# A modulation bias added by a product with the identity, and two SiLUs of keys moved behind the second mixer's values

## The chip, the core and the metric

The kernel runs on one core of a Trainium2 chip. The metric is the device time of one execution in microseconds (us), the median of the runs. The engines are named as in the profile: PE (matrix products; PEld is its weight load), DVE (vector), ACT (scalar functions), POOL (GpSimd) and SP (which issues the DMAs here). Each engine works through its own instructions in order and waits by semaphores for the others.

## What is computed

One layer on 256 latent tokens and 256 context tokens of width 1024: modulation by six vectors from a conditioning vector, two token mixers in parallel (a gated mLSTM with a short convolution on queries and keys, and an HGRN2 scan), a gated merge, and a mixture of experts (top 4 of 32). Cut to what the change touches:

```python
sh1, sc1, g1, sh2, sc2, g2 = split(silu(c) @ w_ada + b_ada, 6)      # late part: g1, sh2, sc2, g2
p = modulate(rmsnorm(x), sh1, sc1) @ w_in + b_in
mqk, mv, mo, hq, hi, hg, hf, ga, gb, mg = split(p)
mq, mk = split(silu(short_conv(mqk, conv_w)))                       # 4 heads each, 3x3 taps
mlstm(mq * 128 ** -0.5, mk, mv, mg)                                 # first mixer
hgrn(silu(hq), (1 - lb) * sigmoid(-hf), hi, log(lb + (1 - lb) * sigmoid(hf)))   # second mixer, 4 heads
```

## The kernel before

**Stages.** The first 280 us or so are the front: norms, the early modulation, and the products with `w_in`, done unit by unit. A unit is a weight tile of 1024 x 256 that is loaded, split into a high and a low part (the high part is the cast L226 on ACT, the low part the subtraction L228 on DVE, for three units on POOL), and multiplied in two blocks by three products each (L237). The units go in the order: queries 2 (first tile done before), `hf` 0, keys 0, `hf` 1, keys 1, `hi` 0, `hi` 1, `hf` 2, `hf` 3, first mixer's values `mv` 0 and 1, then the gates. A block's result stands in a PSUM bank until an engine copies it out; `mm_bank` hands out two banks named `mm` and one named `am` in turn, and only the two `mm` while the late modulation runs. So a block waits until the block two or three before it was copied out. `hi` has four blocks, copied out by DVE at L511.

**Key and query blocks.** `ev_conv` copies a block into an image on ACT and appends its convolution to the list `convs`; a convolution is 9 taps on DVE for queries and 9 + 3 for keys (L661 to L670). After each block the unit loop takes one convolution from `convs`. `silu_qk` (L738) first empties `convs` and then does the SiLU of all four heads of queries and keys: a sigmoid on ACT into `csg`, and a product on DVE (L749 for keys, L751 for queries).

**The second mixer's heads.** `hgrn_head` is a generator for one head; the unit loop advances it block by block, two heads with `hi` and `hf`, two with `mv`. A head runs scans on DVE (L534 to L542), 28 subtractions on DVE into X (L560, L561), the exponentials of X (L562), of G (L543) and of Y (L567 to L569) on ACT, products of Y on POOL (L570 to L572), of X on DVE and POOL (L582, L583), transposes `trh` (L588) and small products on PE. `last_heads` prepares heads 2 and 3: eight sigmoids, then `exp_table` orders the load of the table for exponentials and logarithms, then four logarithms (L516). `to_hgrn` does the same for heads 0 and 1, behind the SiLU.

**The late modulation.** `ada_rest` takes two halves of 8 weight tiles. For each it forms products in the bank `am` (L196), spread over the blocks from `hf` 2 on by the table `rest_at`, and DVE adds the bank to `ada_sb`, which holds the bias (L855). The second half uses the same bank and waits for that addition.

**What sets the order.** Outside the parts under `manual_schedule` the framework's scheduler orders each engine's instructions by its own estimates, so the position of an instruction follows from the built program, not from the text alone.

Of the kernel before, what the change touches and what calls it, by code (L numbers as in the profile page):

```python
# [12 lines left out]
AF = mybir.ActivationFunctionType  # L13
OP = mybir.AluOpType
# [3 lines left out]
P = 128  # L18
D = 1024
KB = 8  # L20
T = 256
NTOK = 512
HM = 4
# [41 lines left out]
def layer_kernel(ctx: ExitStack, tc, x, ctxt, w_ada, b_ada, n_mix_post, n_ffn_post, w_in, b_in, w_pa, w_pb, w_out,  # L65
                 w_router, b_router, w_gu, b_gu, w_dn, b_dn, consts, vecs, out, dbg=None):
    nc = tc.nc
# [13 lines left out]
    def bcast_rows(vec, n):  # L81
# [5 lines left out]
    ident = cp.tile([P, P], F32, name="ident")  # L87
# [35 lines left out]
    ada_sb = ctx.enter_context(tc.tile_pool(name="fa", bufs=1, side="right", reuse_waits="tile")).tile(  # L123
        [P, 2, 512], F32, name="ada_sb")
# [10 lines left out]
    qT = fp.tile([P, HM, T], F32, name="qT")  # L135
    kT = fp.tile([P, HM, NTOK], F32, name="kT")
# [19 lines left out]
    def raw_tile():  # L156
        return ringr.tile([P, 2048], F32, name="w", tag="w", bufs=2)
# [31 lines left out]
    def ada_load(c0, k):  # L189
        w = raw_tile()  # L190
        nc.sync.dma_start(w, w_ada[k * P:(k + 1) * P, c0:c0 + 2048])
        return w

    def ada_mm(bank, w, k):
        for j in range(4):
            nc.tensor.matmul(bank[32 * j:32 * j + 32, :], cs[:, k, :], w[:, 512 * j:512 * j + 512],  # L196
                             start=(k == 0), stop=(k == KB - 1), skip_group_check=True)

    banks = []

    def mm_bank():

        banks.append("mm" if len(banks) % 3 < 2 or ada_runs else "am")
        return pmm.tile([P, 512], F32, name="mm", tag=banks[-1], bufs=2 if banks[-1] == "mm" else 1)
# [78 lines left out]
    def after(instructions):  # L283

        stack = ExitStack()
        for i_ in () if in_order else instructions:
            stack.enter_context(tc.issue_after(i_.ins))
        return stack

    def exp_table(instructions):  # L290

        with after(instructions):
            ld = nc.scalar.preload_act_table_set("natural_log_exp_and_others")
        return after([ld])
# [150 lines left out]
    sig = []  # L445
# [46 lines left out]
    def silu_hq():  # L492
        for j in range(2):
            q2 = hqT[:, 2 * j:2 * j + 2]
            sg = hq_.tile([P, 2, T], F32, name="sg", tag="sg", bufs=1)
            with after(last_xs):
                sig.append(nc.scalar.activation(sg, q2, AF.Sigmoid))
            nc.gpsimd.tensor_tensor(q2, q2, sg, op=OP.mult)
# [16 lines left out]
    def log_f(r):  # L515
        nc.scalar.activation(lf[r], lf[r], AF.Ln, scale=olb[:, r:r + 1], bias=lb[:, r:r + 1])  # L516
        nc.vector.tensor_scalar(kk[r], kk[r], olb[:, r:r + 1], None, op0=OP.mult)

    def last_heads():
        sg2 = []  # L520
        with after(hexp):
            for r in (2, 6, 3, 7):
                sg2.append(nc.scalar.activation(kk[r], lf[r], AF.Sigmoid, scale=-1.0))
                sg2.append(nc.scalar.activation(lf[r], lf[r], AF.Sigmoid))
        estack.append(exp_table(sg2))
        for r in (2, 6, 3, 7):
            log_f(r)
        work.extend(hgrn_head(h) for h in (2, 3))
# [113 lines left out]
    convs = []  # L642
# [92 lines left out]
        nc.scalar.activation(gcol[:, 0:4], tg[:, 0:4], AF.Identity)  # L735
        nc.scalar.activation(gcol[:, 4:8], tg[:, 4:8], AF.Exp)

    def silu_qk():  # L738
        while convs:
            convs.pop(0)()  # L740
        sg = hq_.tile([P, 2, NTOK], F32, name="csg", tag="Y")
        n_ = 0
        for h in range(HM):
            for a, n, sc in ((qT[:, h], T, float(P) ** -0.5), (kT[:, h], NTOK, None)):
                g = sg[:, n_ % 2, 0:n]
                n_ += 1
                sig.append(nc.scalar.activation(g, a, AF.Sigmoid))
                if sc is None:
                    nc.vector.tensor_mul(a, a, g)  # L749
                else:  # L750
                    nc.vector.scalar_tensor_tensor(a, a, sc, g, op0=OP.mult, op1=OP.mult)  # L751

    def ev_v(cc):
        def ev(b, i):
# [90 lines left out]
    def ada_rest():  # L845
        for i in range(8):
            nc.gpsimd.dma_start(ada_sb[32 * (i % 4):32 * (i % 4) + 1, i // 4, :],
                                b_ada[2048 + 512 * i:2560 + 512 * i].rearrange("(a b) -> a b", a=1))
        for hf in range(2):
            b = pmm.tile([P, 512], F32, name="am", tag="am", bufs=1)  # L850
            for k in range(KB):
                ada_mm(b, ada_load(2048 + 2048 * hf, k), k)
                if k < KB - 1:
                    yield
            nc.vector.tensor_add(ada_sb[:, hf], ada_sb[:, hf], b)  # L855
            yield

    def block_of(a, k):
# [46 lines left out]

    def to_hgrn():
        silu_hq()
        silu_qk()
        estack.append(exp_table(sig))
        for r in (0, 4, 1, 5):  # L910
            log_f(r)
# [4 lines left out]
    def to_last():  # L916
        step(100)
        last_heads()
# [7 lines left out]
    for u in (mq_[1], hf_[0], mk_[0], hf_[1], mk_[1]):  # L926
        unit(*u)
    unit(*hi_[0], to_hgrn)
    unit(*hi_[1], None, first_heads)
    unit(*hf_[2])  # L930
# [46 lines left out]
    first = True  # L977
    for c0, n, cnt_ in ((HG, "hg", 2), (MO, "mo", 2), (GA, "ga", 4), (GB, "gb", 4)):
        for cc in range(cnt_):
            unit(win(c0 + 256 * cc), blocks_T(T, ev_gate(n, c0, 2 * cc), ev_gate(n, c0, 2 * cc + 1)),  # L980
                 to_late if first else head_norms if (n, cc) == ("gb", 2) else None)
            first = False
# [107 lines left out]
    def first_merge(i):  # L1090
# [3 lines left out]
              half(w_pb, 0, HM, 512, 512)]  # L1094
    rest_at = {(7, 0): 1, (7, 1): 1, (8, 0): 2, (8, 1): 2, (9, 0): 2, (9, 1): 3, (10, 0): 3, (10, 1): 2}
    rest = ada_rest()
    load_at = {(18, 0): ((first_gu, 0, 0), (first_gu, 0, 1),),
                (19, 0): ((first_gu, 1, 0),),
# [69 lines left out]
    for n_ in range(4):  # L1168
# [20 lines left out]
        g = (gga, ggb)[i]  # L1189
        blks = [slice(4 * q_ + 2 * j2, 4 * q_ + 2 * j2 + 2) for j2 in range(2)]  # L1190
        for j2, blk in enumerate(blks):
            b = mm_bank()
# [11 lines left out]
    a = L["aT"].rearrange("p i a k t -> p (i a k t)")  # L1204
# [641 lines left out]
    with tc.manual_schedule():  # L1846
# [5 lines left out]
        for ch in range(2):  # L1852
            ends[ch]()
            for hf in range(2):
                hs_ = slice(512 * hf, 512 * hf + 512)
                nc.vector.scalar_tensor_tensor(x1[:, ch, hs_], scr[2 * ch + hf], yss[:, 4 + ch:5 + ch], x1[:, ch, hs_],  # L1856
                                               op0=OP.mult, op1=OP.add)
# [48 lines left out]
```

## Time and profile before

| | |
|---|---|
| median of 3 runs | 1363.46 us (1362.53 to 1363.48) |
| profiled execution | 1364.41 us, span 1362.6 us |
| PE busy over the span | 1265.5 us (93%) |
| DVE, ACT, POOL busy | 561.8, 361.8, 129.6 us |
| granted TensorE clock, mean | 0.981 of full speed |
| bytes moved | 474.12 MB, mean 348 GB/s |

The span runs from the first to the last instruction. In a timeline an entry has its start, its length, engine, line, operation and tiles; `x8` means eight instructions in a row, and what stands in square brackets is the idle time of the engine just before, with what ended it. A PE length includes the time in the pipeline, so the next entry can start before the end. Instructions are in pairs on PE for a full fp32 product.

### The profile page before, as it was taken

Reading aid. Unit: us, or ns where it says so; the run is one execution under the profiler, and the core shown is the slowest. Engines: PE = TensorE matmul, PEld = TensorE weight load, DVE = VectorE, ACT = ScalarE, POOL = GpSimd, SP = SyncE. Lnnn points to the kernel's source line nnn. Section 1 sums busy time; section 2 is a strip of 40 time slices with the busy share of each in tenths; the row PEclk is TensorE's granted clock in tenths of the full one; section 3 lists DMA queues with packets and bytes.
Section 4 is the critical chain, followed back from the end, with each engine's and each line's share of the span. In section 5 each row is a group of like instructions: output and inputs, shape, how many; then the busy total and the mean of one; then the engine's idle time right before and its main releaser. Section 6 shows DMA issues by size and latency. Waiting matters only on the chain. (4 is left out here: it accounts for less than half of the span.)

```text
span 1362.6 us, 20982 instructions
## 1 busy us (share of the span) xinstructions
PE 1265.5 (93%) x8719; PEld 637.9 (47%) x8719; DVE 561.8 (41%) x1211; ACT 361.8 (27%) x712; POOL 129.6 (10%) x140
## 2 busy tenths in 40 slices
PE   4998877999998899999999999999999999999995
PEld 2788665799993333333333333333333333333321
DVE  4699477787666332322222222222222222222224
ACT  3557362446643321111111111211121111211102
POOL 4543335300110000000000000000000000000000
PEclk9999988999999899999999999999999999999997
DMA  9731625745889989999999999999999999999994
GB/s 324 242 102 63 202 78 195 260 135 195 309 304 395 390 367 422 430 424 427 427 427 427 425 392 429 426 426 426 429 424 427 426 428 427 425 428 426 427 420 163
DMA packets 78424, 474.12 MB, mean 348 GB/s; under 512 B 6048, under 2 KB 45480, under 8 KB 50672
## 3 DMA queue, kind: packets, MB, share of 16 engines
q1 hardware_dynamic: 77936, 472.54, 85.7%
q8 instruction: 70, 1.15, 0.3%
q14 instruction: 34, 0.28, 0.1%
q0 software_dynamic: 384, 0.15, 0.0%
HBM read 471.60 MB, written 1.07 MB: 347 GB/s over the span
## 5 line engine op out<-in xcount | busy, mean ns | idle before, releaser
L1609 PE MATMUL pg<-wc,hmh 128*64 128x512 f32 x1048 | 271.8, 598 | 14.9 <-DMA wc<-in_w_gu_dram 14.4
L1609 PE MATMUL pu<-wc,hmh 128*64 128x512 f32 x1048 | 268.9, 592 | 0.0
L1659 PE MATMUL dnl<-wc,hmh 128*64 128x512 f32 x1056 | 236.0, 598 | 9.4 <-ACT hmh L1640 9.1
L1659 PEld LDWEIGHTS dnl<-wc,hmh 128*64 128x64 f32 x1056 | 73.6, 137 | 169.1 <-issue 135.4
L1651 DVE TENSOR_TENSOR ys<-dnl,ys 128x512 fp32r<-128x512 f32 x32 | 22.1, 692 | 307.2 <-ACT ys L1650 307.2
L1609 PEld LDWEIGHTS pu<-wc,hmh 128*64 128x64 f32 x1048 | 74.4, 137 | 150.5 <-issue 150.5
L1620 ACT ACTIVATE scr<-scr 128x512 f32<-128x512 f32 (+1 forms) x34 | 21.0, 619 | 465.8 <-DVE scr L1619 465.8
L1609 PEld LDWEIGHTS pg<-wc,hmh 128*64 128x64 f32 x1048 | 66.9, 136 | 145.5 <-issue 107.4
L1675 DVE SCALAR_TENSOR_TENSOR xr<-sc,wv,xr 128x512 f32<-128x512 f32 x124 | 87.4, 747 | 109.5 <-PE sc L1669 109.5
L1619 DVE TENSOR_SCALAR scr<-pg 128x512 f32<-128x512 f32 (+1 forms) x34 | 22.9, 676 | 219.7 <-PE pg L1609 219.7
L237 PE MATMUL mm<-xh,wp 128*128 128x256 f32 (+1 forms) x576 | 107.7, 332 | 4.2 <-DVE hi_sb L511 3.1
L237 PEld LDWEIGHTS mm<-xh,wp 128*128 128x128 f32 x576 | 88.0, 196 | 14.8 <-issue 4.1
L1385 ACT ACTIVATE hmh<-xp,s2c,a2c 128x64 f32<-128x64 f32 x264 | 81.5, 414 | 38.6 <-PE xp L1581 33.2
L1717 POOL TENSOR_TENSOR scr<-xr,g2n 128x512 f32<-128x512 f32 x2 | 2.5, 1266 | 908.2 <-issue 908.2
L1650 ACT CAST ys<-dnl 128x512 fp32r<-128x512 f32 x32 | 18.7, 585 | 232.3 <-PE dnl L1659 232.3
L1581 PEld LDWEIGHTS <-hb 128*128 128x128 bf16 x960 | 43.7, 98 | 24.3 <-issue 24.3
L228 DVE TENSOR_TENSOR wp<-w,wp 128x2048 fp32r<-128x2048 f32 x21 | 48.0, 2288 | 13.4 <-ACT wp L226 13.4
L237 PE MATMUL mm<-xl,wp 128*128 128x256 f32 (+1 forms) x288 | 53.2, 328 | 0.0
L1669 PE MATMUL sc<-ys,ohT 64*128 64x512 f32 x256 | 48.3, 450 | 4.0 <-DVE xr L1673 3.1
L226 ACT CAST wp<-w 128x2048 fp32r<-128x2048 f32 x25 | 47.5, 1900 | 15.6 <-PE mm L237 8.1
L1581 PE MATMUL xp<-oh,hb 128*128 128x64 bf16 x960 | 47.2, 193 | 0.0
L237 PEld LDWEIGHTS mm<-xl,wp 128*128 128x128 f32 x288 | 44.4, 196 | 4.2
(625 smaller groups left out, 1529.4 us busy)
## 6 DMA issues: line engine op xcount, KB each, us to landing
wc<-in_w_gu_dram SPq DMA_DIRECT2D x119, 2048.0 KB, 25.2
wc<-in_w_dn_dram SPq DMA_DIRECT2D x63, 2048.0 KB, 25.2
w<-in_w_in_dram SPq DMA_DIRECT2D x26, 1024.0 KB, 5.3
w<-in_w_ada_dram SPq DMA_DIRECT2D x16, 1024.0 KB, 4.9
wc<-in_w_gu_dram SPq DMA_DIRECT2D x16, 1024.0 KB, 27.0
aw<-in_w_ada_dram SPq DMA_DIRECT2D x8, 1024.0 KB, 11.7
w<-in_w_pa_dram SPq DMA_DIRECT2D x2, 1024.0 KB, 5.3
w<-in_w_out_dram SPq DMA_DIRECT2D x2, 1024.0 KB, 6.6
```

The source lines that it names most:

```text
L226: nc.scalar.copy(hi, w)
L228: eng.tensor_tensor(lo, w, hi.bitcast(F32), op=OP.subtract)
L237: nc.tensor.matmul(o, ls[k][a], rs[k][b], start=(i + k == 0), stop=(i == 2 and k == n - 1))
L1385: nc.scalar.activation(xg[:, k], xp[k], AF.Identity, scale=a2c[:, k:k + 1], bias=s2c[:, k:k + 1])
L1581: nc.tensor.matmul(xp[:, k], part[:, ch, k * P:(k + 1) * P], oh[:, ch], start=(i == 0), stop=(i == 5))
L1609: nc.tensor.matmul(banks[u][n * g:n * g + n, :], xg[:, k], rows_[:, c0:c0 + W], start=False, stop=(k == KB - 1), skip_group_check=True)
L1619: nc.vector.tensor_scalar(g_, cut(banks[0], i), 7.0, None, op0=OP.min)
L1620: nc.scalar.activation(s_, g_, AF.Sigmoid, scale=1.702)
L1651: nc.vector.tensor_sub(ys[1], b, ys[0].bitcast(F32))
L1659: nc.tensor.matmul(b[64 * hf:64 * hf + 64, :], aT_[:, j, g], dn[g][:, j, hf * 512:hf * 512 + 512], start=(g == 0 and j == 0), stop=(g == 1 ...
L1669: nc.tensor.matmul(s[hf], ohT[ps_, ch * P:(ch + 1) * P], ys[i][ps_], start=(i == 0), stop=(i == 1))
L1675: nc.vector.scalar_tensor_tensor(dst, s[hf], wv[:, ch, col:col + 1], dst, op0=OP.mult, op1=OP.add)
```

## The change

1. In `ada_rest` a product of `ada_sb` with the identity (`ident`) opens the accumulation in the bank, so that the bias stands in it; the 8 weight tiles' products add to it, and ACT copies the bank to `ada_sb`. DVE's addition is gone.
2. `silu_qk` takes the heads to be done. `to_hgrn` leaves the last two convolutions in `convs`, and does the SiLU of four queries and of keys 0 and 1. `last_heads` takes what is left in `convs`, and does the SiLU of keys 2 and 3 behind its sigmoids and before the table load.

```diff
-    def ada_mm(bank, w, k):
+    def ada_mm(bank, w, k, first=True):
         for j in range(4):
             nc.tensor.matmul(bank[32 * j:32 * j + 32, :], cs[:, k, :], w[:, 512 * j:512 * j + 512],
-                             start=(k == 0), stop=(k == KB - 1), skip_group_check=True)
+                             start=(first and k == 0), stop=(k == KB - 1), skip_group_check=True)
...
                 sg2.append(nc.scalar.activation(lf[r], lf[r], AF.Sigmoid))
+            while convs:
+                convs.pop(0)()
+            silu_qk((), range(2, HM), sg2)
         estack.append(exp_table(sg2))
...
-    def silu_qk():
-        while convs:
-            convs.pop(0)()
+    def silu_qk(qs, ks, done):
         sg = hq_.tile([P, 2, NTOK], F32, name="csg", tag="Y")
         n_ = 0
-        for h in range(HM):
-            for a, n, sc in ((qT[:, h], T, float(P) ** -0.5), (kT[:, h], NTOK, None)):
+        for a, n, sc in [(qT[:, h], T, float(P) ** -0.5) for h in qs] + [(kT[:, h], NTOK, None) for h in ks]:
...
             b = pmm.tile([P, 512], F32, name="am", tag="am", bufs=1)
+
+            nc.tensor.matmul(b, ident, ada_sb[:, hf], start=True, stop=False, skip_group_check=True)
             for k in range(KB):
-                ada_mm(b, ada_load(2048 + 2048 * hf, k), k)
+                ada_mm(b, ada_load(2048 + 2048 * hf, k), k, False)
                 if k < KB - 1:
                     yield
-            nc.vector.tensor_add(ada_sb[:, hf], ada_sb[:, hf], b)
+            nc.scalar.copy(ada_sb[:, hf], b)
             yield
...
     def to_hgrn():
         silu_hq()
-        silu_qk()
+
+        while len(convs) > 2:
+            convs.pop(0)()
+        silu_qk(range(HM), range(2), sig)
         estack.append(exp_table(sig))
```

**How it moves instructions, first place: the blocks of `hi`.** On DVE, around the copies of `hi` out of PSUM (L511), before:

```order
L749 TENSOR_TENSOR kT<-kT,csg 128x512
L511 TENSOR_TENSOR hi_sb<-mm,bvi 128x2x256
L583 TENSOR_TENSOR xr<-xr,kks 128x8x16
L228 TENSOR_TENSOR wp<-w,wp 128x2048
L534 SCALAR_TENSOR_TENSOR A<-scm_667,lf_659 128x256
L535 SCALAR_TENSOR_TENSOR A<-scm_668,lf_659 128x256
L511 TENSOR_TENSOR hi_sb<-mm,bvi 128x2x256 x2
```

and with the change:

```order
L586 TENSOR_TENSOR xr<-xr,kks 128x8x16
L537 SCALAR_TENSOR_TENSOR A<-scm_667,lf_659 128x256
L538 SCALAR_TENSOR_TENSOR A<-scm_668,lf_659 128x256
L511 TENSOR_TENSOR hi_sb<-mm,bvi 128x2x256
L228 TENSOR_TENSOR wp<-w,wp 128x2048
L511 TENSOR_TENSOR hi_sb<-mm,bvi 128x2x256 x2
```

The product of the last key (L749) is gone from here, and the scans of head 1 (L534, L535; now L537, L538) stand before the second copy instead of before the third. The taps of the last two key blocks keep their place ahead of the first copy.

On POOL in the same stretch, before:

```order
L550 TENSOR_TENSOR ks<-kks 128x256
L545 TENSOR_TENSOR G<-G,kks 128x256 x2
L228 TENSOR_TENSOR wp<-w,wp 128x2048
L582 TENSOR_TENSOR xr<-xr,hqT 128x16x8
L583 TENSOR_TENSOR xr<-xr,kks 128x16x8
```

and with the change:

```order
L553 TENSOR_TENSOR ks<-kks 128x256
L548 TENSOR_TENSOR G<-G,kks 128x256 x2
L573 TENSOR_TENSOR Y<-Y,hqT 128x256
L574 TENSOR_TENSOR Y<-Y,hqT 128x128
L575 TENSOR_TENSOR Y<-Y,kks 128x128
L228 TENSOR_TENSOR wp<-w,wp 128x2048
L573 TENSOR_TENSOR Y<-Y,hqT 128x256
L574 TENSOR_TENSOR Y<-Y,hqT 128x128
L575 TENSOR_TENSOR Y<-Y,kks 128x128
L585 TENSOR_TENSOR xr<-xr,hqT 128x16x8
```

The six products of Y of head 0 stood behind the eight products of X; now three stand before and three behind the split of a weight tile (L228), ahead of the products of X.

**Second place: ACT at the preparation of heads 2 and 3**, before:

```order
L524 ACTIVATE lf_660<-lf_660 128x512
L293 ACT_TABLE_LOAD
L639 ACTIVATE hmh<-ho__1874 128x128
L516 ACTIVATE lf_660<-lf_660,lb,olb 128x512 x2
L639 ACTIVATE hmh<-ho__1880 128x128
L516 ACTIVATE lf_660<-lf_660,lb,olb 128x512 x2
L226 CAST wp<-w 128x2048
L543 ACTIVATE G<-G 128x512
```

and with the change:

```order
L524 ACTIVATE lf_660<-lf_660 128x512
L642 ACTIVATE hmh<-ho__1871 128x128
L747 ACTIVATE csg<-kT 128x512
L642 ACTIVATE hmh<-ho__1877 128x128
L747 ACTIVATE csg<-kT 128x512
L293 ACT_TABLE_LOAD
L516 ACTIVATE lf_660<-lf_660,lb,olb 128x512 x4
L226 CAST wp<-w 128x2048
L546 ACTIVATE G<-G 128x512
```

The table load stood before head 1's two results (`hmh<-ho_`) were copied out; now it stands behind both and behind the two sigmoids of keys, and the logarithms and the cast follow it. On DVE the two products of keys stand directly ahead of the scans of head 2.

**Third place: the change of halves of the late modulation.** PE before:

```order
L237 MATMUL mm<-wp,xh 128x256 x6
L588 MATMUL trh<-ident,G 128x128 x4
L237 MATMUL mm<-wp,xh 128x256 x8
L237 MATMUL mm<-wp,xl 128x256
L196 MATMUL am<-w,cs 32x512 x4
L237 MATMUL mm<-wp,xl 128x256 x7
```

and with the change:

```order
L237 MATMUL mm<-wp,xh 128x256 x6
L591 MATMUL trh<-ident,G 128x128 x3
L852 MATMUL am<-ada_sb,ident 128x512
L591 MATMUL trh<-ident,G 128x128
L237 MATMUL mm<-wp,xh 128x256 x2
L196 MATMUL am<-w,cs 32x512 x4
```

The first instruction that needs the freed bank `am` now stands ahead of nine products of the next block that stood ahead of it before. The copy that frees the bank (L857) stands on ACT like this:

```order
L572 ACTIVATE Y<-A 128x128
L570 ACTIVATE Y<-A 128x256
L571 ACTIVATE Y<-A 128x128
L565 ACTIVATE xr<-xr 128x1792
L857 COPY ada_sb<-am 128x512
L593 ACTIVATE kt<-trh 128x512
```

It stands behind the second exponential of X of head 2 (L565). Before, DVE's addition stood behind the 20 products of X of that head and one scan.

## Rows read from the trace of the kernel before

**Rows 1.** Busy time of the engines by stretch, in us, with the number of instructions: from, to and length; PE, PEld, DVE, ACT, POOL; the granted clock; the share of the DMA engines; GB/s. From the middle of the gates to the last expert.

```profile
290.00:410.00 120.00, 119.67 (x985) 118.31 (x984) 85.11 (x190) 67.50 (x105) 10.12 (x5) 1.00 0.68 243
...
500.00:1330.00 830.00, 805.76 (x4994) 288.02 (x4992) 208.83 (x358) 123.89 (x326) 0.00 (x0) 1.00 1.00 425
```

**Rows 2.** Who waited for whom, PE alone, 100 to 300 us: waiting instruction, what it waited for, us in total, times, longest.

```profile
PE db L624 <- issue: 7.4, 3, 4.6
PE am L196 <- DVE ada_sb L855: 6.3, 1, 6.3
PE mm L237 <- DVE hi_sb L511: 5.4, 2, 3.1
...
PE mm L237 <- DVE wp L228: 1.2, 1, 1.2
```

**Rows 3.** Timeline of PE: a block of `hf` 1 (24 products, 16 and 8), the fourth block of `hi`, the first block of `hf` 2, and the first product of the late modulation behind it.

```profile
97.88 3.79 PE L237 MATMUL mm<-xh,wp 128*128 128x512 f32 x16
101.51 1.98 PE L237 MATMUL mm<-xl,wp 128*128 128x512 f32 x8
...
131.82 1.88 PE L237 MATMUL mm<-wp,xh 128*128 128x256 f32 x8 [2.33 <-DVE hi_sb L511]
...
142.43 3.60 PE L237 MATMUL mm<-xh,wp 128*128 128x512 f32 x8 [3.10 <-DVE hi_sb L511]
...
149.64 1.06 PE L196 MATMUL am<-w,cs 128*32 128x512 f32 x8
```

**Rows 4.** Busy time by stretch (columns as in rows 1) around the two waits for `hi` and behind the wait for the late modulation.

```profile
80.00:120.00 40.00, 38.77 (x203) 33.31 (x202) 40.00 (x86) 28.27 (x37) 12.40 (x5) 1.00 0.26 79
...
132.00:135.50 3.50, 3.50 (x18) 3.50 (x19) 3.50 (x19) 3.45 (x4) 2.92 (x1) 0.51 0.00 0
...
142.30:145.70 3.40, 3.27 (x8) 2.62 (x9) 2.81 (x2) 0.00 (x0) 3.40 (x4) 0.50 0.56 236
...
217.00:224.50 7.50, 5.39 (x25) 3.73 (x26) 4.77 (x12) 0.63 (x1) 6.76 (x11) 0.54 0.32 102
```

**Rows 5.** Timeline of DVE between the first and the third copy of `hi` out of PSUM.

```profile
131.07 0.69 DVE L511 TENSOR_TENSOR hi_sb<-mm,bvi 128x512 f32<-128x512 f32 x1
131.67 0.48 DVE L663 SCALAR_TENSOR_TENSOR kT<-xr,cols,kT 128x256 f32<-128x256 f32 x1
132.06 0.29 DVE L582 TENSOR_TENSOR xr<-xr,hqT 128x128 f32<-128x128 f32 x1
...
135.90 0.70 DVE L749 TENSOR_TENSOR kT<-kT,csg 128x512 f32<-128x512 f32 x1
...
137.70 2.29 DVE L228 TENSOR_TENSOR wp<-w,wp 128x2048 fp32r<-128x2048 f32 x1 [0.20 <-ACT wp L226]
139.91 0.94 DVE L534 TENSOR_TENSOR_SCAN A<-scm,lf 128x256 f32<-128x256 f32 x1
...
141.63 1.26 DVE L511 TENSOR_TENSOR hi_sb<-mm,bvi 128x512 f32<-128x512 f32 x2
```

**Rows 6.** Timeline of ACT in the same stretch: the sigmoid of a key (start, length).

```profile
133.81 0.63 ACT L747 ACTIVATE csg<-kT 128x512 f32<-128x512 f32 x1
```

**Rows 7.** Timeline of POOL, 114 to 137 us and 208 to 214 us.

```profile
118.38 4.81 POOL L228 TENSOR_TENSOR wp<-w,wp 128x2048 fp32r<-128x2048 f32 x1 [2.06 <-ACT wp L226]
132.58 4.35 POOL L582 TENSOR_TENSOR xr<-xr,hqT 128x128 f32<-128x128 f32 x1 [9.39 <-ACT xr L562]
...
202.21 6.64 POOL L228 TENSOR_TENSOR wp<-w,wp 128x2048 fp32r<-128x2048 f32 x1 [5.91 <-ACT wp L226]
208.81 1.52 POOL L545 TENSOR_TENSOR G<-G,kks 128x256 f32<-128x256 f32 x2
...
213.19 0.50 POOL L572 TENSOR_TENSOR Y<-Y,kks 128x128 f32<-128x128 f32 x1
```

**Rows 8.** Timeline of DVE at the scans and subtractions of head 2: the first scan, the subtraction that meets POOL's split, the last one (the eighth behind it), and the addition of the late modulation.

```profile
198.10 0.69 DVE L534 TENSOR_TENSOR_SCAN A<-scm,lf 128x256 f32<-128x256 f32 x1
...
204.94 4.07 DVE L561 TENSOR_TENSOR xr<-A 128x128 f32<-128x128 f32 x1
...
213.29 0.54 DVE L561 TENSOR_TENSOR xr<-A 128x128 f32<-128x128 f32 x1
...
218.39 0.67 DVE L855 TENSOR_TENSOR ada_sb<-ada_sb,am 128x512 f32<-128x512 f32 x1
```

**Rows 9.** Timeline of ACT from the table load of heads 2 and 3 to the second exponential of X of head 2.

```profile
194.11 1.28 ACT L293 ACT_TABLE_LOAD   x1
...
198.65 0.28 ACT L639 ACTIVATE hmh<-ho__1880 128x128 f32<-128x128 f32 x1 [0.41 <-PE ho__1880 L638]
198.83 1.51 ACT L516 ACTIVATE lf<-lf,lb,olb 128x512 f32<-128x512 f32 x2
200.24 1.89 ACT L226 CAST wp<-w 128x2048 fp32r<-128x2048 f32 x1
...
213.87 1.70 ACT L562 ACTIVATE xr<-xr 128x1792 f32<-128x1792 f32 x1 [7.00 <-DVE xr L561]
```

**Rows 10.** Timeline of PE: the first products behind head 2's transposes, the first product of the late modulation's second half, and a later product of 128 rows by 128 with 256 columns.

```profile
211.49 1.20 PE L237 MATMUL mm<-wp,xh 128*128 128x256 f32 x8
...
219.11 1.94 PE L196 MATMUL am<-w,cs 128*32 128x512 f32 x8 [6.30 <-DVE ada_sb L855]
...
267.83 1.02 PE L775 MATMUL sA<-qT,kT 128*128 128x256 f32 x4
```

More of the change, by code (lines that the diff above doesn't have):

```diff
@@ L736, in gates @@
         nc.scalar.activation(gcol[:, 4:8], tg[:, 4:8], AF.Exp)
-    def silu_qk():
-        while convs:
-            convs.pop(0)()
+    def silu_qk(qs, ks, done):
         sg = hq_.tile([P, 2, NTOK], F32, name="csg", tag="Y")
         n_ = 0
-        for h in range(HM):
-            for a, n, sc in ((qT[:, h], T, float(P) ** -0.5), (kT[:, h], NTOK, None)):
[L745 to L751, printed above, removed]
+        for a, n, sc in [(qT[:, h], T, float(P) ** -0.5) for h in qs] + [(kT[:, h], NTOK, None) for h in ks]:
+            g = sg[:, n_ % 2, 0:n]
+            n_ += 1
+            done.append(nc.scalar.activation(g, a, AF.Sigmoid))
+            if sc is None:
+                nc.vector.tensor_mul(a, a, g)
+            else:
+                nc.vector.scalar_tensor_tensor(a, a, sc, g, op0=OP.mult, op1=OP.mult)
     def ev_v(cc):
```

## The prediction

> **What bounds the kernel now.** I read the busy time by stretch first. From 500 to 1330 us the DMA engines move data the whole time (share 1.00, 425 GB/s), and from 290 to 410 us PE is busy 119.67 of 120 us [rows 1]. Neither stretch holds an instruction of the change. The experts' weights start to load when the front's buffers come free, so I let a shift of the front pass one to one to the end; the only question is how far the front, up to about 280 us, moves. There PE has holes, and the waits of PE name them [rows 2]: 6.3 us for DVE's addition of the late modulation (L855), 5.4 us in two waits for the copies of `hi` (L511), 1.2 us for a low part (L228). The 7.4 us put down to nothing ("issue") I can't derive; I leave them unchanged and let them widen the range.
>
> The next view is the clock. After the 2.33 us wait at 131.82 [rows 3] the granted clock of 132 to 135.5 us is 0.51 of full speed, after the 3.10 us wait at 142.43 it is 0.50, after the 6.30 us one 0.54 over 217 to 224.5 us. [...] In 80 to 120 us, which holds the wait of 1.2 us, it stays at 1.00 [rows 4]. So a long wait is paid twice. The first block of `hf` 2 shows the price: from 142.43 to 149.64 it takes 7.21 us for 24 products, where 16 such products take 3.63 us at full clock (97.88 to 101.51), so 24 take 5.44. Half the clock costs 1.77 us there [rows 3].
>
> DVE decides the waits for `hi`: in 80 to 120 us it is busy 40.00 of 40 us [rows 4], so what stands ahead of a copy of `hi` on DVE delays that copy.
>
> **The blocks of hi.** The text says that the last convolutions move. The order shows that they don't: the unit loop still takes one per block, and their taps stay ahead of the first copy. Only the SiLU of two keys leaves.
> - First copy (131.07): one product of a key goes (0.60: L749 is as long as the copy, 0.70, and behind the copy the next one starts 0.60 later), one tap (0.40, from 131.67 to 132.06) and one product of X (0.20) come ahead of it [rows 5]. The net is nothing.
> - Third copy (141.63): I walk on from 131.67 without the tap and without L749: 19 products of X, which take 132.06 to 135.90 now, 3.84; the two scans, 139.91 to 141.63, 1.72; one copy, 0.60; the split, 137.70 to 139.91, 2.21. That ends at 140.0, so the third copy is 1.6 us earlier [rows 5].
> - Against it: six products of Y on POOL, which stood far behind, now run while DVE is full. What that costs shows later: behind the subtraction that ends at 209.0, eight more on DVE take until 213.8, 4.8 us, where the products of X take 0.20 each; the same time holds eight instructions of POOL, two on G and six on Y (208.81 to 213.69) [rows 5, 7, 8]. So 4.8 - 1.6 = 3.2 us were added, 0.40 per instruction, and six cost 2.4 us. From below: nothing, because at 132.58 POOL's product of X took 4.35 us while DVE went on at 0.20 [rows 5, 7]. From above: the whole length of the six, 210.33 to 213.69, 3.4 us [rows 7]. I take 2.4, which is the same instructions against the same kind.
> - Both copies get these 2.4 us if the products lie ahead of the first: that comes at 133.5, the third at 141.63 - 1.6 + 2.4 = 142.4, 0.8 us late (bounds -1.6 and +1.8).
> - PE: the 1.2 us wait for the low part goes, which only lengthens the wait for the first copy, to 2.33 + 1.2 + 2.4, about 6 us. The fourth block then runs from 134.2. It ended at 142.43 - 3.10 = 139.33 [rows 3]; I add 2.4, and 0.5 because the half clock behind the wait of 6.3 us covered some 5 us instead of 3.5 [rows 4] (an estimate). It ends at 142.2, and `hf` 2 can start at 142.43 + 0.8 = 143.2. The wait is 1.0 us, under the 1.2 us that left the clock at 1.00. So the 1.77 us go (bound: they stay).
>
> The front stands at 0.8 - 1.77 = **-1.0 us** at 149.6. (Both bounds together: -3.4 and +1.8.)
>
> [...]
>
> **The product with the identity.** The first stands on PE right where the late modulation begins (149.64), in a stretch without waits. Two products of 128 rows by 128 with 256 columns took 1.02 us with the pipeline's 0.17 [rows 10], the same number of columns in the same type: **+0.85 us**, bounds 0.7 and 1.0. The copy on ACT (L857) in place of the addition on DVE (L855) has no one waiting in the first half that would not wait anyway.
>
> **The change of halves.** Before, the bank `am` came free with L855, which ran at 218.39 behind 20 products of X. In the new order it comes free with the copy L857 on ACT, directly behind the second exponential of X of head 2, which ran at 213.87 [rows 8, 9]. By itself that is some 3 us earlier. But that exponential is itself late:
> - The table load ran at 194.11, while ACT waited for head 1's results anyway. Now two sigmoids, the load and all four logarithms stand behind the second result, 198.65. From 198.83: a sigmoid, 0.6 [rows 6], the load, 1.28, one logarithm, 0.75 (1.51 for two) [rows 9]: the scans of head 2 start at 201.5 instead of 198.10, 3.4 us late. The cast, which POOL's split waits for, moves from 200.24 to 203.6, as far; so the split meets the subtractions as before, and the second exponential is at 213.87 + 3.4 = 217.3.
> - Copy done: 217.3 + 1.6 + 0.6 = 219.5, where L855 ended at 219.06 [rows 8, 9]. PE goes on 0.45 us later than at 219.11.
> - Behind that wait now stand the product with the identity (0.85), a transpose (0.1) and nine products of the next block, which ran ahead of it, from 211.49 to 212.66, 1.17 us [rows 10].
>
> Together **+2.6 us**. From below: without POOL's 3.2 us on the subtractions, -0.6. The half clock behind this wait stays in either case. DVE's 0.6 us without L855 are worth nothing; it idles soon after.
>
> **Sum.** -1.0 + 0.85 + 2.6 = **+2.45 us** on the profiled execution (1364.41 us, which lies 0.95 over the median of 1363.46). On the median: **1365.9 us**. A measurement of this kernel can tell 0.2%, 2.7 us, from no change, so this forecast reads as no change, close to the edge.
>
> **Rivals.**
> - *Slower.* POOL reaches the six products of Y late, behind its split, so that they meet DVE between the first and the third copy of `hi` and hold it for their full length. Then the fourth block is not shifted, the third copy is 1.8 us late, and PE waits longer than now before `hf` 2, so the half clock stays. It decides once the fourth block ends more than 2 us ahead of the third copy. For it: the split took 4.81 us at 118.38 [rows 7], and three of the six stand behind it. Price: 1.8 + 0.85 + 2.6 = +5.3, 1368.7 us.
> - *Faster.* POOL waits for DVE, not the other way, in both places, as at 132.58. Then the third copy is 1.6 early and the clock stays up, -3.4; with the product, +0.85, and the change of halves at its lower bound, -0.6, that makes -3.1: 1360.3 us. Against it: the eight subtractions from 209 on show DVE slowed by these very instructions.
> - *Little moves.* The first wait takes everything and `hf` 2 keeps its half clock and its start; only 0.85 and part of 2.6 come: +1 to +3.5, inside or at the edge of the forecast's 0.2%.
>
> **Chances.** No change that can be told 0.45, the forecast with the third rival's lower half; slower 0.41, the slower rival and those outcomes of the forecast in which a bound of +0.3 or more is reached; faster 0.14. The range runs from close to the faster rival to the slower one: 1360.8 to 1368.7 us.
>
> **What would show it.** In the changed profile: a wait of about 6 us ahead of the fourth block of `hi`, one of about 1 us ahead of `hf` 2, and a granted clock near 1.00 in that block, 5.4 us long. POOL's products of Y between 115 and 127 us with slow instructions of DVE beside them. An identity product of 0.85 us ahead of L196. Scans of head 2 at about 201, and PE waiting for ACT's copy until about 219. I am wrong if the clock is at half in `hf` 2, if the copy lands before 216, or if the experts' stretch doesn't shift with the front.

## The result, and the profile after

The changed kernel takes 1370.39 us (median; 1369.79 to 1374.22) where the kernel before takes 1363.48 in the same measurement: a ratio of 1.0054 (95% interval 1.0036 to 1.0073). It is slower, by 6.9 us; the forecast was 1365.9, its range ended at 1368.7. The profiled execution is the median one, 1370.39 us, with a span of 1368.5 and a mean granted clock of 0.977 (before 1362.6 and 0.981).

The waits of PE, 100 to 300 us, in the changed kernel (columns as in [rows 2]):

```profile
PE db L627 <- issue: 9.2, 3, 4.5
PE trh L591 <- POOL G L548: 5.9, 1, 5.9
PE mm L237 <- DVE hi_sb L511: 5.7, 1, 5.7
```

The two waits for `hi` have become one, the wait for the low part (L228) is gone, and the wait for DVE's addition (L855) too. In its place PE waits as long for POOL's products on G, and the pauses without a named cause ("issue": the engine waited for nothing that the profile shows) have grown from 7.4 to 9.2 us. Where these stand, from PE's timeline (fourth block of `hi`, first block of `hf` 2 and the first identity product; the change of halves; the products `db` of the last head):

```profile
131.76 2.07 PE L237 MATMUL mm<-wp,xh 128*128 128x256 f32 x8 [5.69 <-DVE hi_sb L511]
...
140.52 2.08 PE L237 MATMUL mm<-xh,wp 128*128 128x512 f32 x8 [1.13 <-ACT wp L226]
...
146.07 1.02 PE L852 MATMUL am<-ada_sb,ident 128*128 128x512 f32 x2
147.03 1.06 PE L196 MATMUL am<-w,cs 128*32 128x512 f32 x8
...
214.94 1.21 PE L591 MATMUL trh<-ident,G 128*128 128x128 f32 x3 [5.90 <-POOL G L548]
215.94 1.99 PE L852 MATMUL am<-ada_sb,ident 128*128 128x512 f32 x2
...
219.01 1.91 PE L196 MATMUL am<-w,cs 128*32 128x512 f32 x8 [0.44 <-DMA w<-in_w_ada_dram]
...
254.12 0.76 PE L627 MATMUL db<-xr 128*32 128x32 f32 x62
258.53 0.38 PE L627 MATMUL db<-xr 128*32 128x32 f32 x10 [3.65 <-issue]
```

Busy time by stretch (columns as in [rows 1], the granted clock is the third from the end): the fourth block of `hi`, the first block of `hf` 2, one stretch ahead of the pause, one that holds its start, and one behind the front.

```profile
132.00:135.50 3.50, 3.50 (x17) 3.50 (x18) 3.50 (x19) 1.63 (x1) 3.50 (x1) 0.51 0.00 0
140.50:146.00 5.50, 5.48 (x24) 4.57 (x25) 2.69 (x2) 0.00 (x0) 3.55 (x4) 1.00 0.91 283
...
252.50:254.50 2.00, 2.00 (x152) 1.46 (x149) 0.00 (x0) 0.73 (x2) 2.00 (x4) 1.00 0.92 270
254.50:256.00 1.50, 0.38 (x40) 0.26 (x30) 1.19 (x4) 0.46 (x1) 1.07 (x2) 1.00 1.17 375
...
425.00:432.00 7.00, 6.50 (x18) 2.03 (x18) 5.58 (x33) 3.21 (x11) 0.00 (x0) 0.54 0.96 410
```

The block of `hf` 2 runs at a granted clock of 1.00 now (before, 0.50 from 142.3 to 145.7, [rows 4]), the first identity product starts 3.57 us earlier than the late modulation did (146.07, 149.64 in [rows 3]), and until the front's last head the changed kernel is ahead. To see where it falls behind, I matched PE's products one by one between two traces and took the median difference of their start times. In us, against the first profile of the kernel before; the columns are places in that profile, the rows kernels (those of the experiments are named below). Two profiles of one kernel differ too: by up to 2.7 us at 100 us, and by 0.4 to 1.1 us from 150 to 400 us.

```
at (us)                           100   150   200   225   262   290   400   440   495
changed kernel                   -3.6  -2.6  -2.3  -0.7   2.8   2.6   2.7   5.6   6.1
changed kernel, 2nd profile      -3.2  -2.2  -1.5   0.1   3.7   3.7   3.7   5.0   6.2
before, 2nd profile              -2.7  -1.0  -0.5  -1.0  -0.4  -0.4  -0.4   1.1   1.8
part 1 (identity) alone          -1.1   1.2   1.5   0.5   4.1   3.5   3.5   7.4   7.9
part 1, PE's program shifted     -0.5   1.8  -1.2  -1.6   0.3  -0.5  -0.5   1.1   1.7
part 2 (SiLU) alone              -1.6  -3.1  -2.5  -1.4  -0.9  -1.2  -1.2   0.4   0.9
changed, PE's program shifted    -2.2  -1.3  -2.5  -1.8  -1.4  -1.2  -1.1   0.3   0.8
before, PE's program shifted     -2.1   0.5  -1.7  -1.8  -0.8  -1.0  -1.0   0.5   1.0
before, split on DVE             -2.7  -1.0  -2.4  -9.7  -9.7 -10.6 -10.6  -9.2  -8.3
part 1 + split on DVE            -3.0  -0.6  -0.3  -7.8  -3.2  -4.0  -4.0  -2.6  -2.2
changed, split on DVE            -1.5  -0.6  -1.4  -1.6   2.2   2.0   4.5   6.0   6.4
changed, split on DVE, shifted   -1.2  -0.2  -2.7  -2.6   0.0  -0.6   1.9   1.9   2.4
part 2 + split on DVE            -1.4  -2.8  -3.7 -11.1  -9.0  -8.8  -8.8  -8.8  -8.8
```

The first row is the answer in short: -0.7 us where the whole change is through (225), then +3.5 between 225 and 262, and +2.9 near 425, where PE's granted clock is 0.54 from 425 to 432 us.

### The profile page after: what moved, and what is told of

It reads as the page before. It is cut to its first block, busy times and chain, and to the rows that moved or that the text cites. A ratio compares the mean times of both kernels' runs of the same rounds, so it can differ in the third digit from the quotient of the medians.

```text
span 1368.5 us, 20984 instructions
## 1 busy us (share of the span) xinstructions
PE 1268.8 (93%) x8723; PEld 637.0 (47%) x8723; DVE 559.0 (41%) x1209; ACT 356.4 (26%) x709; POOL 135.5 (10%) x140
## 3 DMA queue, kind: packets, MB, share of 16 engines
q8 instruction: 70, 1.15, 0.3%
HBM read 471.60 MB, written 1.07 MB: 345 GB/s over the span
## 5 line engine op out<-in xcount | busy, mean ns | idle before, releaser
L228 DVE TENSOR_TENSOR wp<-w,wp 128x2048 fp32r<-128x2048 f32 x21 | 48.1, 2290 | 24.8 <-ACT wp L226 24.7
L1674 PEld LDWEIGHTS sc<-ys,ohT 64*128 64x128 f32 x256 | 19.6, 186 | 56.2 <-issue 24.3
```

The lines of the kernel that those rows point to most:

```text
L228: eng.tensor_tensor(lo, w, hi.bitcast(F32), op=OP.subtract)
L1674: nc.tensor.matmul(s[hf], ohT[ps_, ch * P:(ch + 1) * P], ys[i][ps_], start=(i == 0), stop=(i == 1))
```

## What the pause in the last head is

At 254.9 us PE stops in the middle of a run of small products (`db`, 128 rows, 32 columns), 3.65 us without a wait that the profile shows. Numbering the entries of PE's program as the trace has them, weight loads included, the pauses stand at entries 1985 and 2497 in both kernels, and the new one at 4033: 1985 + 512 and 1985 + 2048. The DMA view counts packets on a queue "instruction" (q8: 70 packets, 1.15 MB, 16,384 bytes each) beside the data, and each pause ends 2 to 3 us after the start of such a packet. At entry 4033 the two kernels differ in when that packet comes. From the trace's records (us; the pause is from start to start):

```
                      w_in load   PE at entry  instruction  PE at entry  pause at
                      issued      3777         packet       4033         entry 4033
before                253.46      253.41       253.47       255.88       0.53
before, 2nd profile   253.37      253.35       252.56       255.57       0.00
changed               251.40      252.78       255.89       258.53       3.85
changed, 2nd profile  252.52      253.90       256.91       259.45       3.65
```

Before, the next weight tile of `w_in` is asked for when PE is at entry 3777, and the DMA engines are still free (share 0.03); after, 1.4 us earlier, and they are full (share 0.92) when PE comes there. The rows of SP's queue, and of the DMA share, first the kernel before:

```profile
253.46 2.48 SPq L210 DMA_DIRECT2D w<-in_w_in_dram  x2
```

```profile
252.50:254.50 2.00, 2.00 (x155) 1.47 (x149) 0.39 (x2) 0.43 (x1) 2.00 (x4) 1.00 0.03 8
```

and the changed kernel (its stretches are shown above):

```profile
251.40 3.35 SPq L210 DMA_DIRECT2D w<-in_w_in_dram  x2
```

That load waits for a group of the late modulation's products (SP's wait for `am`, L196, up to 4.7 us before and 4.0 after). Before, the group stood among the `db` products (252.29 to 253.37); in the new order it stands ahead of them (250.27 to 251.34). The packets follow PE's entries: 70 of them over 17,532 entries in the kernel before, one for some 250. So the reading is: the next packet of PE's program comes behind 1 MB of weights, 3.1 us behind entry 3777 instead of 0.06, and PE, which otherwise goes from there to entry 4033, 256 entries on, in 2.2 to 2.5 us (before), runs dry for 3.65 us.

In all five profiles that hold part 1 of the change without a shift of PE's program (below), the load was issued 1.2 to 1.9 us ahead of entry 3777, and the packet started 2.5 to 3.5 us behind that entry. In the five without part 1 and without a shift the load came at most 0.1 us behind the entry, and the packet at most 0.24 us behind it. No run moved the load alone, so that the packet waits for the load is read from these times. Just behind the pause, from 259 to 261.5 us, the granted clock is 0.50 as well.

## The experiments

The kernel before is measured with each run; its median was 1363.4 to 1364.7.

**Part 1 alone** (`ada_mm(..., first=False)`, the identity product, the copy on ACT; `silu_qk` as before).

> Part 1 of the change alone (product with the identity, copy on ACT). Theory of the sum: the blocks of hi stay as before (waits of 2.3 and 3.1 us, half clock in the first block of hf 2), +0.95 us for the first identity product (it took 0.96 us from start to start in the changed kernel), and at the change of halves the bank comes free behind the second exponential of X, about 216 instead of 219.06, -2.9, while 0.95 and the nine products of 1.17 us stand behind the wait: -0.8. Together about 0, 1363 to 1364.5. Theory of late effects (a pause of PE in the db products, a fall of the clock near 425 us, both set by when things fall and not by the work): the same up to 235 us, and behind it steps of 2 to 4 us that the sum does not have, if the instruction block's end in the db products or the fall of the clock moves.

1370.39 us, ratio 1.0048 (1.0030 to 1.0066): the whole loss. The sum holds to 225 us (+0.5, expected about 0), and the bank came free when it said, 216.4:

```profile
216.47 2.07 PE L852 MATMUL am<-ada_sb,ident 128*128 128x512 f32 x2 [3.66 <-ACT ada_sb L857]
```

Then the pause at entry 4033 is 3.83 us; the load stood at 252.57, entry 3777 at 253.95, the packet at 257.13.

**Part 2 alone** (`silu_qk` as changed, the addition on DVE kept).

> Part 2 alone (SiLU of keys 2 and 3 behind the second mixer's values). Theory of the sum: the first block of hf 2 starts 1.9 us earlier and runs at full clock, -3.6 by 150 us; POOL's split at 202 waits for DVE (11 us instead of 6.6) and PE waits for POOL's G and then for the late modulation's bank, which gives back 2 to 4 us: 1360 to 1364. Theory of late effects: the same up to 235 us, then a pause of up to 4 us in the db products of the last head, because two weight loads start earlier and the instruction fetch waits behind them, and 2.9 us more if the clock falls near 425 us: 1366 to 1371.

1363.89 us, 1.0002 (0.9989 to 1.0014): no change. -3.1 by 150 us, about as expected, of which the wait for POOL's G (5.0 us) gives back 1.7 by 225; no pause (0.65; load 252.55, entry 3777 at 252.51). So the pause came with part 1, not with an earlier front, as my expectation had it.

**PE's program shifted**: 32 products of the identity into an unused corner of a bank,

```diff
+        for _ in range(32):
+            nc.tensor.matmul(tcol[:, 0, 0:32], ident, ident[:, 0:32], start=True, stop=True)
```

which move every later entry by 128 and leave the order of all engines as it is.

> The changed kernel with 32 small products (128 entries of PE's program) at the very start, where PE waits for its first weights; the order of all engines is the same otherwise. Theory of late instruction fetch: the pauses of 4.5, 1.0 and 3.65 us in the db products at 166, 190 and 255 us stand exactly where a block of 512 entries or half of it ends; shifted by 128 entries the ends leave those places or are fetched before the weight loads start, and the pauses fall under 0.6 us each: 3 to 9 us faster than the changed kernel, 1361 to 1367. Rival, that the pause is a wait for data that the profile does not show: nothing changes at those places, 1370 +- 1.

> The kernel before with the same 32 small products at the very start. Late instruction fetch: its pauses of 4.59 and 2.46 us at 169 and 192 us go, 2 to 7 us faster, 1356 to 1361. Rival (a wait for data): 1363.5 +- 1.

1373.57 (1.0074) and 1367.78 us (1.0036), both slower: a miss, since the products were not hidden. They cost 13.7 us on the spot, each with a weight load of 128 columns; of this 3.2 us stayed in the changed kernel's time and 4.4 in that of the kernel before. The pauses themselves did go from entries 1985 and 2497, but the kernel before got one of 3.2 us at 237 us. So I put them where PE waits for weights, as `bank[0:32, 0:32]` from `ident[:, 0:32]` in the first `ada_a`:

> The changed kernel with the same shift of PE's program by 32 small products (here of 32 rows and columns), now behind the first transposes, where PE waits for its weights anyway, so that the start costs nothing. Late instruction fetch: the pause of 3.85 us at 255 us goes, and with it at least the 2.5 us that the first shift left net of its own start: 1367 to 1368.5 at the changed kernel's clock (0.977). Rival, that what the pause covers costs the same without it: 1370 to 1371.5.

> The kernel before with the same hidden shift. Its pauses of 4.6 and 2.5 us in the db products go, but with the costly start those came back by 240 us as other waits, and a pause of 3.2 us came at 234: 1362 to 1364.5, no change. Rival, that each pause is paid in full: 1356 to 1358.

1367.30 us (1.0022, 1.0010 to 1.0034) and 1364.90 (1.0011, 1.0001 to 1.0021). The changed kernel wins 3.1 us, the kernel before loses 1.3, though its pauses of 4.6 and 2.5 us left it as well: what they covered is waited for elsewhere by 225 us, and it got pauses of 2.98 and 1.07 us at entries 3521 and 4033 (234.50 and 254.57 us). In the changed kernel, `db` of the last head without a pause:

```profile
253.09 0.86 PE L629 MATMUL db<-xr 128*32 128x32 f32 x76
254.77 0.81 PE L629 MATMUL db<-xr 128*32 128x32 f32 x70
```

Entry 3777 was passed at 249.41, the packet came at 249.00, the load at 251.29. An edit whose products nobody reads and which leaves the order of all engines takes the step between 225 and 262 us from 3.5 down to 0.4 us: that this step is the pause, and that the pause hangs on the place in the program, is shown.

**The split at 202 us on DVE.** In the changed kernel POOL needed 11.56 us for it (6.64 before, [rows 7]), and its products on G, for which PE waits, came behind it:

```profile
202.60 11.56 POOL L228 TENSOR_TENSOR wp<-w,wp 128x2048 fp32r<-128x2048 f32 x1 [9.23 <-ACT wp L226]
214.12 1.50 POOL L548 TENSOR_TENSOR G<-G,kks 128x256 f32<-128x256 f32 x2
```

DVE went on at 0.20 us per instruction up to its copies out of PSUM (L757, 209.72); the product behind these took 3.92 us, and the split ended at 214.16, 4.44 us behind the start of the copies:

```profile
209.72 0.75 DVE L757 TENSOR_TENSOR v_sb<-mm,bvi 128x256 f32<-128x256 f32 x2
210.38 3.92 DVE L585 TENSOR_TENSOR xr<-xr,hqT 128x128 f32<-128x128 f32 x1
```

```diff
-    on_pool = (5, 7, 11)
+    on_pool = (5, 7)
```

> The changed kernel with the split of the weight tile at 202 us on DVE instead of POOL (there it took 11.56 us, since DVE's stream of products with two inputs in SBUF ran first). Theory that POOL waits for DVE there: the split takes 2.3 us on DVE, POOL's products on G come some 8 us earlier, PE's wait of 5.9 us for G goes, and 2 to 4 us are won by 235 us; behind that the late pause and the clock may take other values: 1364 to 1369. Rival, that DVE is the bound there and pays 2.3 us more: 1370 to 1373.

> Part 2 alone (the SiLU moved, DVE's addition kept) with the same split on DVE: POOL's wait goes, PE's second wait is then set by DVE's addition of the late modulation alone. If the wait for POOL was the bound: 2 to 4 us under part 2 alone, 1360 to 1362. If the addition behind the products of X is: 1363 to 1365.

> The kernel before with the split of the weight tile at 202 us on DVE alone; PE's order is the same. If the win of part 2 with this split (1357.9) comes from the split, about the same time here: 1357 to 1360. If it needs the SiLU moved as well: 1362 to 1365.

Changed kernel 1372.32 (1.0065), part 2 alone 1357.94 (0.9960, 0.9944 to 0.9976), kernel before **1357.50** (0.9955, 0.9942 to 0.9969). The first is a miss: its time lies in the rival's range, but PE still waited for POOL, which is not the rival's cause. The last two beat both kernels, and the kernel before needs nothing of the change for it. In the kernel before with this split DVE's subtractions from 199.87 to 206.57 us take 0.28 to 0.29 us each (one took 4.07, [rows 8]), and it adds the late modulation (L855) at 208.79 instead of 218.39 [rows 8], and where PE waited 6.3 us ahead of L196 it now waits 0.39 ahead of two transposes:

```profile
209.52 0.44 PE L588 MATMUL trh<-ident,G 128*128 128x128 f32 x2 [0.39 <-DVE ada_sb L855]
...
210.95 1.06 PE L196 MATMUL am<-w,cs 128*32 128x512 f32 x8
```

In the changed kernel the two products on G now met DVE's stream in place of the split, and PE waited 4.60 us for them (in the kernel before they took 9.12 us from 200.35, and were done by 209.5):

```profile
203.95 12.27 POOL L548 TENSOR_TENSOR G<-G,kks 128x256 f32<-128x256 f32 x2 [9.76 <-DVE xr L563]
```

> The changed kernel with that split on DVE and the hidden shift of PE's program. Late instruction fetch: the pause of 3.97 us that the split alone left at 254 us goes, 3 to 4 us under it: 1368 to 1369.5. Rival: 1372.

1367.13 us (1.0030, 1.0020 to 1.0039), 5.2 under the same kernel without the shift: the pause of 3.97 us was gone again. It is not all of the 5.2: in the table 1.0 us of the lead stands at 225 us already, and as a pause of 2.45 us came at entry 3521 (233.06), the step up to 262 us only fell from 3.8 to 2.6.

**The clock near 425 us.** Is its fall the change's? Both kernels once more, unchanged:

> The kernel before once more, for a second profile. If the fall of PE's clock near 425 us belongs to the changed kernel: none here. If it is a matter of when the stretch falls in an execution: it may be here too, and the time of an execution follows its mean clock, some 0.7 us for each 0.001.

> The changed kernel once more, for a second profile. The pause of 3.85 us is there again at the same entry of PE's program (it follows from the order and from the weight load's start); the fall of the clock near 425 us may be there or not.

1364.19 us (0.9996) and 1371.62 (1.0059). The fall is in the second profile of the kernel before too; the first row is of its first profile, the second of the second:

```profile
425.00:430.00 5.00, 5.00 (x24) 1.69 (x26) 4.45 (x25) 2.30 (x9) 0.00 (x0) 1.00 0.93 364
```

```profile
419.00:424.00 5.00, 3.44 (x11) 0.71 (x9) 2.61 (x12) 0.37 (x1) 0.00 (x0) 0.75 1.02 433
```

In the table, from 400 to 440 us, the same instructions cost 0 or 1.5 us more in the kernel before, 2.9 or 1.3 in the changed one, 3.9 in part 1 alone. The granted clock of 400 to 440 us goes with it, in this order 1.00, 0.96, 0.91, 0.96 and 0.87. The 2.9 us of the first profile are therefore no price of the change that one profile could show.

**What part 1 costs without the pause, and without the wait.**

> Part 1 alone with the hidden shift of PE's program by 128 entries. If the pause in the db products (3.83 us in part 1 alone) is what part 1 costs: 3 to 4 us under part 1 alone (1370.4), 1366.5 to 1367.5, within 3 us of the shifted kernel before (1364.9). If the product with the identity costs by itself what part 1 costs: 1370 or more.

> Part 1 on top of the kernel before with the split at 202 us on DVE (1357.5), where PE no longer waits long at the change of halves. If the price of part 1 is its two products (0.96 us each) and nothing else: 1358.5 to 1360.5. If it brings the early weight load and the pause again: 3 to 4 us more, 1362 to 1364. If it brings the wait for POOL's products on G again (as in the changed kernel with this split): 1367 or more.

Part 1 with the shift: 1365.74 us (1.0008, 0.9995 to 1.0021), 4.65 under part 1 alone and 0.8 over the shifted kernel before. Neither is a bare price. Of the lead over part 1 alone the table has 2.1 us at 225 us already, where the two other pauses are gone, and 1.7 from the step up to 262; and the shifted kernel before has pauses of 2.98 and 1.07 us that this one has not. Part 1 on the kernel with the split on DVE: 1363.59, which is 6.1 over that kernel. Its pause is back (load 245.48, entry 3777 at 247.37, packet 249.87):

```profile
248.72 0.75 PE L624 MATMUL db<-xr 128*32 128x32 f32 x62
252.47 0.28 PE L624 MATMUL db<-xr 128*32 128x32 f32 x10 [3.00 <-issue]
```

From the table: 1.9 us of it by 225 us, which is about the price of two products of 0.96, and 4.6 more by 262 us. Of these the pause is 2.5 (3.19 against 0.73 us); behind a wait of 1.54 us for POOL's Y (L572) the granted clock of 243.2 to 246.4 us is 0.50 as well, where it is 1.00 from 225 to 262 us in the kernel with the split alone. So the products' own price is small, and up to 400 us the pause is the largest single part wherever part 1 stands without the shift.

## Why the prediction was wrong, step by step

- **The step that failed** is the first paragraph's: the pauses "put down to nothing", which I left unchanged and meant to let widen the range, though the range's ends are the two rivals' and hold nothing for them. One of them, in the last head, went from 0.33 to 3.65 us. I counted the change's instructions and not the loads that its order releases. Without the pause the shifted kernel gives 1367.3 us, inside the range. At 400 us itself the sum looks right by luck: it had +2.45 behind the change of halves, the trace has -0.7 there, and the pause takes it to +2.7. What is left of the miss comes behind 400 us (the last two points).
- **The blocks of hi**: forecast -1.0 us by 149.6 with bounds -3.4 and +1.8; measured -3.6, past the better bound. The clock term was right: the wait ahead of `hf` 2 is 1.13 us, the clock 1.00, the block 5.55 us long. The wait ahead of the fourth block is 5.69, forecast about 6. The term for POOL's products of Y was not: the six products do slow DVE (0.83 instead of 0.34 for a tap at 114.47), but the first copy is at 131.02, where it was (131.07), because the instructions ahead of them ran earlier: the tap that meets POOL's split (4.84 us in both kernels) starts at 116.43 instead of 118.63. The third copy is 1.9 us early (139.69), at my bound of -1.6 and beyond.
- **The product with the identity**: +0.85 forecast, 0.96 measured (146.07 to 147.03).
- **The change of halves**: +2.6 forecast, +1.9 measured (-2.6 at 150, -0.7 at 225), and the size hides a wrong mechanism. I let POOL's split meet DVE's subtractions as before and hold them. It began just after DVE's copies from PSUM (202.60 behind L757 at 201.98) instead of before them (202.21 and 204.27), DVE's stream behind it ran at 0.20 us per instruction, and the split took 11.56 us instead of 6.64: the scans of head 2 began at 198.64, not 201.5, the copy L857 was done at 209.6, not 219.5 (before 216, which the prediction names as a sign of being wrong), and PE waited for POOL's G instead. Part 1 alone, where POOL's split is not moved, freed the bank at 216.4, where the sum for that run put it.
- **One to one to the end**: right where nothing else comes in; from 290 to 400 us the difference stays at 2.6 to 2.7. That the end holds a fall of the clock of its own, different from one execution to the next (granted from 400 to 440 us: 1.00 and 0.96 before, 0.91 and 0.96 after), I had not seen, and the range had no room for it.
- **What stays open**: at 400 us the two profiles of each kernel are on average 3.4 us apart (2.7 and 3.7 against 0 and -0.4), the medians 6.9. It is the same without the pause: with the shift the profiles of the two kernels stand level at 400 us (-1.1 and -1.0), and the medians are 2.4 us apart. Most of the rest goes with the clock: within a kernel an execution with 0.001 less mean clock takes about 0.6 us more (an estimate from all executions; single kernels give 0.3 to 1.4, the shifted kernel before no slope), and seven executions of the changed kernel average 0.978, 22 of the kernel before 0.982, which makes some 2.3 us. Why the changed kernel meets low clocks more often the runs don't settle. Part 1 with the shift has low ones too (0.9775 on average) at 1365.7 us; in which stretches they lie is not shown.

## What to carry to other kernels

Ask of an edit not only what it adds to each engine, but which transfers its new order starts earlier, and what else they are in front of: here 1 MB of weights, asked for 1.4 us ahead of PE's entry 3777, and a packet of PE's own program 3.1 us behind that entry. A pause "without a cause" at a fixed spacing of program entries is worth a count of the entries; a few dozen hidden small products tell whether it hangs on the place in the program. And before a wait is worked around, look at what makes the awaited engine late: with POOL's split moved to DVE, the 6.3 us wait that the change was built around goes by itself, and 6 us with it.

## What the hardware showed that I had not expected

- At one entry of its program, 4033, PE paused 3.2 to 4.0 us from start to start in the five profiles where a packet of 16,384 bytes on the queue "instruction" started 2.5 to 3.5 us behind entry 3777, with a load of 1 MB issued ahead of it (DMA share 0.92 in the changed kernel). In the eleven where the packet came ahead of that load or at most 0.2 us behind it the pause was 0 to 1.50 us.
- The same subtraction of 128 x 2048 took POOL from 4.64 to 11.56 us in the changed kernel alone. Around 202 us it ended 4.58 us behind the start of DVE's copies out of PSUM (L757) before, and 4.44 us in the changed kernel: there the copies came 7.12 us behind its start (202.60, 209.72), before 2.06 us (202.21, 204.27). DVE's instruction behind the copies took 4.07 us before [rows 8] and 3.92 in the changed kernel, where those ahead of them ran at 0.20.
- The same stretch of PE's work, 400 to 440 us, cost 0 to 3.9 us more in one profile than in another, with granted clocks of 1.00 to 0.87.
